# Rotary embedding over 16 heads: three matmul rows per tile in place of four, a new order of the first loads, and one last store

## Chip, cores, metric

One core of one Trainium2 chip. The metric is the device time of one execution in microseconds (us), median of several. A span is the time from the first to the last instruction in a trace of one execution; the device time of an execution was 1.8 us (kernel before) to 2.2 us (changed kernel) above its span. All runs quoted are fast, that is, none was over 1.5% above the fastest run of its kernel. The granted clock is the share of its full clock that TensorE was allowed, as the trace records it.

## The reference

Input x is 16 x 512 x 1024 fp32 (33.5 MB), seen as 16 heads of 64; cos and sin are 512 x 32.

```python
x = x.reshape(batch, seq, num_heads, head_dim)
x1, x2 = x[..., :half_dim], x[..., half_dim:]
rotated = concatenate([x1*cos - x2*sin, x1*sin + x2*cos], axis=-1)
```

So each output element is one product with cos plus one with a signed sin of the swapped half. Every byte is read once and written once: 67.1 MB.

## The kernel before

Eight tiles of 128 partitions x 8192 floats; a tile has eight "rows" k of 1024 floats per partition. Five tiles are buffered. For each row, POOL (GpSimd) makes `b` = swapped x times signed sin; VectorE (DVE) makes x times cos. The sum is made in one of two ways: in a matmul row, TensorE (PE) adds `b` onto the product in PSUM (the memory that matmuls accumulate in) by a multiplication with the identity and ScalarE (ACT) copies the sum back; in any other row DVE adds. In `own` rows DVE makes the sine product itself, in place, and PE adds that.

```python
PE_ROWS = (0, 2, 4, 6)          # matmul rows
DVE_B = ((0,), (0, 4))          # own rows in even and odd tiles
FIRST = (3, 8)                  # pieces of the first tile's load
LAST_OUT = (4, 8)               # pieces of the last tile's store
# ... (cut: views, pools)
load(0, 0, FIRST[0])
# sin table, then cos table (64 KB each), then the rest of tile 0, then tiles 1 to 4
# ... (cut)
nc.tensor.matmul(out=sin_t, lhsT=spread, rhs=sin_sb, start=True, stop=True)
nc.tensor.matmul(out=cos_t, lhsT=spread, rhs=cos_sb, start=True, stop=True)
nc.vector.tensor_scalar_mul(out=sns[:, :, 0, :], in0=sin_k, scalar1=-1.0)
nc.vector.tensor_copy(out=sns[:, :, 1, :], in_=sin_k)
# ... (cut: two more small sine copies)
for t in range(NT):
    for k in range(KK):
        r = xt[:, k * dim : (k + 1) * dim]
        own = k in DVE_B[t % 2]
        if not own:
            nc.gpsimd.tensor_tensor(out=halves(b), in0=swapped(r, nh), in1=over_heads(sk), op=ALU.mult)
        if k in PE_ROWS:
            nc.vector.tensor_tensor(out=pairs(ps), in0=pairs(r), in1=cos_b(k), op=ALU.mult)
            # own: DVE sine product in place; then two fp32 matmuls with the identity into ps
            nc.scalar.copy(out=r, in_=ps)
            while pending: add()
        else:
            while pending: add()
            nc.vector.tensor_tensor(out=pairs(ps), in0=pairs(r), in1=cos_b(k), op=ALU.mult)  # ps from pd, one buffer
            pending.append((r, ps, b))       # DVE's add comes later
    while pending: add()
    # store(t); the last tile in the pieces of LAST_OUT; loads of tiles 5 to 7 follow the store of tile 2
```

All loads and stores are issued by SyncE (SP) in the order loads 0 to 4, stores 0 to 2, loads 5 to 7, stores 3 to 7, on one queue (q1 of the profile, kind hardware_dynamic: 67.24 of the 67.28 MB). In the trace they landed in that order: store 0 at 62.4 us, store 2 at 82.3, load 5 at 92.0, load 7 at 111.4, store 3 at 122.0, store 6 at 150.9 and the second half of store 7 at 160.5.

Of the kernel before, what the change touches and what calls it, by code (L numbers as in the profile page):

```python
# [14 lines left out]
B_BUFS = 6  # L15
BANK = 512

PE_ROWS = (0, 2, 4, 6)

DVE_B = ((0,), (0, 4))  # L20

FIRST = (3, 8)
LAST_OUT = (4, 8)

SIN_PARTS = (64,)
COS_PARTS = (64,)


@with_exitstack
def kernel(  # L30
# [13 lines left out]
    nc = tc.nc  # L44
# [12 lines left out]
    cos_v = cos.rearrange("(p k) j -> p (k j)", k=KK)  # L57
    sin_v = sin.rearrange("(p k) j -> p (k j)", k=KK)
# [12 lines left out]
    def load(t, lo=0, hi=KK):  # L71
        if tiles[t] is None:
            tiles[t] = xp.tile([P, F], FP32, name="xt")
        s = slice(lo * dim, hi * dim)
        nc.sync.dma_start(out=tiles[t][:, s], in_=x_v[t][:, s])  # L75

    def store(t, lo=0, hi=KK):
        s = slice(lo * dim, hi * dim)
        nc.sync.dma_start(out=out_v[t][:, s], in_=tiles[t][:, s])

    load(0, 0, FIRST[0])
    sin_sb = bp.tile([P, dim], FP32, name="b")[:PB, : KK * half]
    cos_sb = bp.tile([P, dim], FP32, name="b")[:PB, : KK * half]
    for sb, v, parts in ((sin_sb, sin_v, SIN_PARTS), (cos_sb, cos_v, COS_PARTS)):
        lo = 0
        for hi in parts:
            nc.sync.dma_start(out=sb[lo:hi, :], in_=v[lo:hi, :])
            lo = hi
    for lo, hi in zip(FIRST, FIRST[1:]):
        load(0, lo, hi)  # L90
    for t in range(1, BUFS):
        load(t)
# [21 lines left out]
    nc.vector.tensor_copy(out=sns[:, :, 1, :], in_=sin_k)  # L114
    on_dve = sorted(set(DVE_B[0]) | set(DVE_B[1]))
    sns_t = tab[:, KK * half : KK * half + len(on_dve) * hd]
# [7 lines left out]
    def over_heads(s):  # L124
        return bass.AP(tensor=s.tensor, offset=s.offset, ap=[s.ap[0], [0, nh], [1, hd]])

    def swapped(r, n):
        return bass.AP(
            tensor=r.tensor, offset=r.offset + half, ap=[r.ap[0], [hd, n], [-half, 2], [1, half]]
        )  # L130
# [12 lines left out]
    def halves(r):  # L143
        return r.rearrange("p (h a j) -> p h a j", a=2, j=half)
# [7 lines left out]
    for t in range(NT):  # L152
        xt = tiles[t]
# [4 lines that stand above are left out]
                b = bp.tile([P, dim], FP32, name="b")  # L158
                sk = sns[:, k].rearrange("p a j -> p (a j)")
                nc.gpsimd.tensor_tensor(out=halves(b), in0=swapped(r, nh), in1=over_heads(sk), op=ALU.mult)  # L160
            if k in PE_ROWS:
                ps = pe.tile([P, dim], FP32, name="ps")
# [3 lines left out]
                for c in range(0, dim, BANK):  # L166
                    rhs = swapped(r[:, c : c + BANK], BANK // hd) if own else b[:, c : c + BANK]
                    nc.tensor.matmul(  # L168
                        out=ps[:, c : c + BANK], lhsT=ident, rhs=rhs, start=False, stop=True, skip_group_check=True
# [14 lines left out]
        else:  # L184
            lo = 0
            for hi in LAST_OUT:
                store(t, lo, hi)
                lo = hi
# [38 lines left out]
```

## Time and profile before

| what | value |
|---|---|
| time, median (first 3 runs) | 163.11 us |
| span of the profiled run | 161.6 us |
| moved | 67.28 MB, 416 GB/s over the span |
| busy: DVE, POOL, PE, ACT | 128.9, 121.0, 81.8, 33.7 us |
| first DVE row product / last DVE add ends | 10.96 / 142.96 us |
| last store issued / span ends | 143.03 / 161.6 us |

In the slices of the profile each digit is the busy share of one fortieth of the span in tenths. A line of a group or a timeline names source line, engine, operation, output<-input; in brackets stands the idle time before it and what ended it. `xt` is a tile of x, `b` a sine product, `ps` and `pd` are the PSUM buffers of matmul rows and of other rows, `tab` and `sns` hold the tables; SPq is SyncE's instruction queue. In a table of stretches the columns are the stretch, its length, busy us (and count) of PE, weight loads, DVE, ACT and POOL, then granted PE clock, DMA share and GB/s. The lines themselves are in the prediction.

### The profile page before, as it was taken

What the parts mean: (1) busy time and instruction counts of PE and PEld (TensorE: products, weight loads), DVE (VectorE), ACT (ScalarE), POOL (GpSimd) and SP (SyncE); (2) the same over time, 40 slices, a digit from 0 to 9 for tenths busy, and PEclk for the clock granted to TensorE, in tenths of its full rate; (3) what the DMA queues carried; (4) which work ended last, traced back from release to release, by engine and by line L of the source; (5) the groups of instructions that cost most, each with busy time, mean ns of one, the idle gap of its engine ahead of it and who ended that gap; (6) DMA issues with size and microseconds to landing.
All of it is one profiled execution on the core that took longest, in us unless ns stands there. A gap on an engine that the chain in (4) does not pass through costs nothing.

```text
span 161.6 us, 692 instructions
## 1 busy us (share of the span) xinstructions
PE 81.8 (51%) x136; PEld 30.3 (19%) x136; DVE 128.9 (80%) x115; ACT 33.7 (21%) x33; POOL 121.0 (75%) x58
## 2 busy tenths in 40 slices
PE   4136946496429742955097419660984194600000
PEld 1112301241114211311032114210321131100000
DVE  1059897999999989999999999999999999930000
ACT  0003242023302430223113302222223122220000
POOL 1049999999999999999994199999999997000000
PEclk9999996559975998799969965999689879995555
DMA  5999999999999999999999999999999999999992
GB/s 189 395 441 435 454 454 389 446 462 389 438 470 389 389 446 464 389 454 446 397 454 446 397 448 446 406 454 438 406 450 438 406 448 438 414 454 389 438 426 118
DMA packets 2756, 67.28 MB, mean 416 GB/s; under 512 B 320, under 2 KB 448, under 8 KB 448
## 3 DMA queue, kind: packets, MB, share of 16 engines
q1 hardware_dynamic: 2752, 67.24, 97.5%
q8 instruction: 1, 0.02, 0.0%
q14 instruction: 3, 0.02, 0.0%
HBM read 33.69 MB, written 33.55 MB: 416 GB/s over the span
## 4 chain that ended last, share of the span: by engine, by line
DVE 37%; PE 18%; issue 17%; POOL 6%; ACT 4%; DMA 4%; SPq 0%; DVEq 0%; ACTq 0%; POOLq 0%
PE ps L168 17%; DVE xt L150 12%; DVE pd L178 12%; DVE ps L163 7%; POOL b L160 6%; DVE xt L165 5%; ACT xt L171 4%; DMA b<-in_sin_dram 4%; PE tab L110 1%; PE tab L111 1%; DVE tab L118 0%; DVE sns L113 0%; SPq L75 0%; DVE sns L114 0%; DVEq L150 0%
## 5 line engine op out<-in xcount | busy, mean ns | idle before, releaser
L160 POOL TENSOR_TENSOR b<-xt,sns 128x1024 f32<-128x1024 f32 x52 | 120.3, 2350 | 14.5 <-DVE sns L114 9.2
L168 PE MATMUL ps<-xt,ident 128*128 128x512 f32 x48 | 35.8, 888 | 39.2 <-issue 24.5
L171 ACT COPY xt<-ps 128x1024 f32<-128x1024 f32 x32 | 32.4, 1012 | 95.2 <-PE ps L168 90.8
L168 PE MATMUL ps<-b,ident 128*128 128x512 f32 x80 | 43.5, 674 | 14.7 <-DVE ps L163 12.1
L150 DVE TENSOR_TENSOR xt<-pd,b 128x1024 f32<-128x1024 f32 x32 | 39.0, 1218 | 2.2 <-POOL b L160 1.1
L163 DVE TENSOR_TENSOR ps<-xt,tab 128x1024 f32<-128x1024 f32 x32 | 39.1, 1223 | 1.5 <-ACT xt L171 1.3
L178 DVE TENSOR_TENSOR pd<-xt,tab 128x1024 f32<-128x1024 f32 x32 | 39.3, 1227 | 0.8
L168 PEld LDWEIGHTS ps<-b,ident 128*128 128x128 f32 x80 | 17.1, 227 | 44.1 <-issue 30.6
L168 PEld LDWEIGHTS ps<-xt,ident 128*128 128x128 f32 x48 | 11.6, 267 | 58.8 <-issue 46.1
L165 DVE TENSOR_TENSOR xt<-xt,tab 128x1024 f32<-128x1024 f32 x12 | 14.6, 1220 | 0.4
L113 DVE TENSOR_SCALAR sns<-tab 128x256 f32<-128x256 f32 x1 | 0.4, 425 | 8.0 <-PE tab L111 8.0
L171 ACT ACT_TABLE_LOAD x1 | 1.3, 1283 | 13.5 <-DVE xt L165 13.5
L110 PE MATMUL tab<-b,spread 64*128 64x256 f32 x2 | 1.2, 697 | 4.5 <-DMA b<-in_sin_dram 4.5
L101 PE MATMUL ps<-zero 128*128 128x512 bf16 x4 | 1.9, 625 | 1.2 <-DVE zero L97 1.2
L110 PEld LDWEIGHTS tab<-b,spread 64*128 64x128 f32 x2 | 0.5, 308 | 5.4 <-issue 5.4
L111 PE MATMUL tab<-b,spread 64*128 64x256 f32 x2 | 1.1, 631 | 0.0
L97 DVE MEMSET zero<- 128x256 uint32 x1 | 0.3, 272 | 0.9 <-PEq L208 0.9
L101 PEld LDWEIGHTS <-zero 128*128 128x128 bf16 x4 | 0.4, 129 | 1.7 <-DVE zero L97 1.2
L111 PEld LDWEIGHTS tab<-b,spread 64*128 64x128 f32 x2 | 0.7, 333 | 0.2
L118 DVE COPY tab<-sns 128x64 f32<-128x64 f32 x2 | 0.5, 228 | 0.1
L109 DVE COPY spread<-ident 64x64 f32<-64x64 f32 x2 | 0.3, 182 | 0.2 <-POOL ident masks.py:199 0.2
masks.py:197 POOL MEMSET ident<- 128x128 f32 x1 | 0.2, 204 | 0.3 <-POOLq L208 0.3
(6 smaller groups left out, 1.1 us busy)
## 6 DMA issues: line engine op xcount, KB each, us to landing
xt<-in_x_dram SPq DMA_DIRECT2D x7, 4096.0 KB, 29.5
out_dram<-xt SPq DMA_DIRECT2D x7, 4096.0 KB, 30.3
out_dram<-xt SPq DMA_DIRECT2D x2, 2048.0 KB, 18.1
xt<-in_x_dram SPq DMA_DIRECT2D x1, 2560.0 KB, 11.3
xt<-in_x_dram SPq DMA_DIRECT2D x1, 1536.0 KB, 6.2
b<-in_sin_dram SPq DMA_DIRECT2D x1, 64.0 KB, 6.3
b<-in_cos_dram SPq DMA_DIRECT2D x1, 64.0 KB, 6.1
```

The lines of the kernel that those rows point to most:

```text
L101: nc.tensor.matmul(out=ps[:, c : c + BANK], lhsT=zero[:, :P], rhs=zero, start=True, stop=True)
L110: nc.tensor.matmul(out=sin_t, lhsT=spread, rhs=sin_sb, start=True, stop=True)
L111: nc.tensor.matmul(out=cos_t, lhsT=spread, rhs=cos_sb, start=True, stop=True)
L113: nc.vector.tensor_scalar_mul(out=sns[:, :, 0, :], in0=sin_k, scalar1=-1.0)
L118: nc.vector.tensor_copy(out=sns_t[:, i * hd : (i + 1) * hd], in_=sns[:, k])
L150: nc.vector.tensor_tensor(out=r, in0=ps, in1=b, op=ALU.add)
L160: nc.gpsimd.tensor_tensor(out=halves(b), in0=swapped(r, nh), in1=over_heads(sk), op=ALU.mult)
L163: nc.vector.tensor_tensor(out=pairs(ps), in0=pairs(r), in1=cos_b(k), op=ALU.mult)
L165: nc.vector.tensor_tensor(out=halves(r), in0=halves(r), in1=swapped_signed(k), op=ALU.mult)
L168: nc.tensor.matmul(out=ps[:, c : c + BANK], lhsT=ident, rhs=rhs, start=False, stop=True, skip_group_check=True)
L171: nc.scalar.copy(out=r, in_=ps)
L178: nc.vector.tensor_tensor(out=pairs(ps), in0=pairs(r), in1=cos_b(k), op=ALU.mult)
```

## The change

The rows that go over PE fall from four to three, the pieces of the first load are made smaller with the tables placed between them (seemingly to let work start sooner), and the last tile is stored whole.

```diff
-PE_ROWS = (0, 2, 4, 6)
-DVE_B = ((0,), (0, 4))
-FIRST = (3, 8)
-LAST_OUT = (4, 8)
-SIN_PARTS = (64,)
-COS_PARTS = (64,)
+PE_ROWS = (0, 3, 6)
+DVE_B = ((0,), (0, 3))
+FIRST = (2, 4, 8)
+LAST_OUT = (8,)
@@ after load(0, 0, FIRST[0]) and the two table buffers
-    for sb, v, parts in ((sin_sb, sin_v, SIN_PARTS), (cos_sb, cos_v, COS_PARTS)):
-        ... (one DMA each)
-    for lo, hi in zip(FIRST, FIRST[1:]):
+    nc.sync.dma_start(out=sin_sb, in_=sin_v)
+    load(0, FIRST[0], FIRST[1])
+    nc.sync.dma_start(out=cos_sb, in_=cos_v)
+    for lo, hi in zip(FIRST[1:], FIRST[2:]):
         load(0, lo, hi)
```

More of the change, by code (lines that the diff above doesn't have):

```diff
@@ L83 @@
     cos_sb = bp.tile([P, dim], FP32, name="b")[:PB, : KK * half]
-    for sb, v, parts in ((sin_sb, sin_v, SIN_PARTS), (cos_sb, cos_v, COS_PARTS)):
-        lo = 0
-        for hi in parts:
-            nc.sync.dma_start(out=sb[lo:hi, :], in_=v[lo:hi, :])
-            lo = hi
-    for lo, hi in zip(FIRST, FIRST[1:]):
+    nc.sync.dma_start(out=sin_sb, in_=sin_v)
+    load(0, FIRST[0], FIRST[1])
+    nc.sync.dma_start(out=cos_sb, in_=cos_v)
+    for lo, hi in zip(FIRST[1:], FIRST[2:]):
         load(0, lo, hi)
```

## The prediction

> **What bounds the kernel now.** I read the page's slices first, because a kernel that only loads, rotates and stores must be either limited by its transfers or by its busiest engine.
>
> ```profile
> DVE  1059897999999989999999999999999999930000
> POOL 1049999999999999999994199999999997000000
> PEclk9999996559975998799969965999689879995555
> DMA  5999999999999999999999999999999999999992
> ```
>
> VectorE (DVE) is busy 80% of the span but does nothing in the last four and a half slices (some 18 us); the transfers are at 9 in every slice but the first and the last. So the bound is transfers: 67.28 MB at about 430 GB/s. The page's chain of waits gives 37% to DVE and 17% to PE; it ends with the last add at 142.96 us and says nothing of the 18.6 us after it, so I don't take it for the bound.
>
> Next the waits of the DMA queue's own engine, and the busy table of chosen stretches:
>
> ```profile
> SPq L79 <- DVE xt L150: 111.5, 8, 21.0
> SPq L75 <- DMA out_dram<-xt: 19.9, 3, 9.8
> SPq L222 <- DMA out_dram<-xt: 17.1, 1, 17.1
> ```
> ```profile
> 143.00:158.60 15.60, 0.00 (x0) 0.00 (x0) 0.00 (x0) 0.00 (x0) 0.00 (x0) 0.57 0.98 419
> 148.90:158.60 9.70, 0.00 (x0) 0.00 (x0) 0.00 (x0) 0.00 (x0) 0.00 (x0) 0.50 0.99 422
> 100.00:143.00 43.00, 24.53 (x44) 8.55 (x43) 41.92 (x36) 12.14 (x12) 36.15 (x16) 0.91 1.00 433
> ```
>
> The last store is issued at 143.03 and the queue then waits 17.1 us for it. Summing the GB/s after 143 us in 1 us pieces gives 6.62 MB still to move. One tile is 4.19 MB, so 2.43 MB of tile 6 is still ahead of tile 7's first byte: at 425 GB/s that takes 5.7 us, to about 148.8 us. That is the number on which everything turns: **the queue runs dry at about 149 us unless tile 7 has been issued by then**. Before, its last half was issued 6 us (plus its first half, 5 us more) ahead of need.
>
> Last, the pace of DVE in tile 7 (start, duration; steps are start to start) and the start of the program:
>
> ```profile
> 126.11 1.22 DVE L163 TENSOR_TENSOR ps<-xt,tab 128x1024 f32<-128x1024 f32 x1
> 127.36 1.22 DVE L165 TENSOR_TENSOR xt<-xt,tab 128x1024 f32<-128x1024 f32 x1
> 128.50 1.22 DVE L178 TENSOR_TENSOR pd<-xt,tab 128x1024 f32<-128x1024 f32 x1
> 129.63 1.22 DVE L163 TENSOR_TENSOR ps<-xt,tab 128x1024 f32<-128x1024 f32 x1
> 130.76 1.22 DVE L150 TENSOR_TENSOR xt<-pd,b 128x1024 f32<-128x1024 f32 x1
> 132.01 1.23 DVE L178 TENSOR_TENSOR pd<-xt,tab 128x1024 f32<-128x1024 f32 x1
> ...
> 140.40 1.23 DVE L178 TENSOR_TENSOR pd<-xt,tab 128x1024 f32<-128x1024 f32 x1
> 141.74 1.22 DVE L150 TENSOR_TENSOR xt<-pd,b 128x1024 f32<-128x1024 f32 x1
> ```
> ```profile
> 7.57 1.19 PE L110 MATMUL tab<-b,spread 64*128 64x256 f32 x2 [4.49 <-DMA b<-in_sin_dram]
> ...
> 8.55 1.06 PE L111 MATMUL tab<-b,spread 64*128 64x256 f32 x2
> 9.65 0.42 DVE L113 TENSOR_SCALAR sns<-tab 128x256 f32<-128x256 f32 x1 [8.02 <-PE tab L111]
> ...
> 10.96 1.23 DVE L163 TENSOR_TENSOR ps<-xt,tab 128x1024 f32<-128x1024 f32 x1
> ```
>
> The reader sees four kinds of step: 1.14 us to an instruction that needs nothing of the one before; 1.25 to a product that overwrites pd just after the add that read it; 1.26 from the cosine product to the in-place sine product of the same row; 1.34 from a product in pd to the add that reads it at once. At the start, the first sine copy (L113) waits for the matmul of the cos table (L111), not for that of the sine table that it reads.
>
> [...] the trace has 1215 to 1230 for all four groups. So a further add is no cheaper than a product. [...] the trace has 433 in mid-run[...]. Here the first load (1.57 MB) lands 6.2 us after its issue at 0.73; at the 418 GB/s of those microseconds its bytes take 3.76, so 2.4 us are fixed[...]. In a full queue this hides behind the neighbour; behind an empty queue it is paid.
>
> **The change, part by part.**
>
> *Rows.* A row on PE costs DVE one product; a row off PE costs a product and an add. Rows on PE go from (0,2,4,6) to (0,3,6): one more add per tile, 8 in all. The rows whose sine product DVE does itself stay at one in even and two in odd tiles, so that group stays at 12 and POOL at 52. PE loses 16 of its 128 accumulating matmuls and ACT 8 of 32 copies; neither sets the end. In DVE's new order (even tile: product, own sine product, then product, add, product, product, add, product, add, product, product, add, product, add) I count the steps:
> - Before, even: 8 x 1.14 + 3 x 1.25 + 1.26 + 1.34 = 15.47; odd has one own product more, 1.26: 16.73. Tile 7 by this rule ends 16.81 after its start; measured 142.96 - 126.11 = 16.85.
> - After, even: 6 x 1.14 + 4 x 1.25 + 1.26 + 3 x 1.34 = 17.12; odd 18.38. With two neighbouring rows off PE the add follows its own product at once, three times per tile and not once: so a tile costs 1.65 more, not one bare 1.14.
> - Four pairs: before 4 x 32.20 = 128.8, after 4 x 35.50 = 142.0.
>
> Before, the real walk from 10.96 to 142.96 has 132.0, 3.1 above the count: 1.45 in tile 0 (waits for POOL and ACT), the rest spread. POOL makes a product each 2.31 us; in tile 0 after the change its row 7 is ready some 16.2 us after its start, and DVE wants it at about 16.4 after that same moment. So I expect little waiting there, and 0.3 us in all.
>
> *Start.* The cos table lands at 1.75 + 6.1 = 7.85 now, behind 1.57 MB of x. After, it stands behind 2.10 MB: 0.52 MB / 0.42 = 1.25 us later, so 9.1. The sine table is sooner by the same, but L113 will still wait for the cos matmul if the waits are as now (the built program's waits are the same). Then 0.12 + about 1.1 for the matmul, 10.3; the four copies and gaps take 1.31 (9.65 to 10.96), so the first product starts at 11.65: 0.7 later. The smaller first piece gains nothing as DVE has nothing to do without the tables.
>
> *DVE's end.* 11.65 + 142.0 + 0.1 (the last one's duration in place of its step) + 0.3 = about 153.9, against 142.96.
>
> *The tail.* The queue is dry from 148.9. The last tile now goes in one store of 4.19 MB, issued at 153.95. 2.4 fixed + 4.19/0.42 = 10.0 gives landing at 166.3; the span ends 1.1 after the landing (160.5 to 161.6 now): 167.4. Time less span is 163.11 - 161.6 = 1.5, so 168.9. [...] I take 168.8. Dropping the split of the last tile costs nothing before, but here it means that 2 MB that are ready about 9 us earlier wait for the rest.
>
> **The rivals.** (a) All stays hidden: transfers remain the bound, 163.1, perhaps less by a few tenths for a smoother start. For it: 97.5% of transfer time, and 18 us of idle DVE at the end. Against: those 18 us consist of 6 of earlier backlog and 10 of the tile itself, so slack is 6, and the count says 11. It would need the extra add to be eaten by waits now there; only 3.1 us of them exist. (b) The naive count: 8 adds x 1.14 = 9.1, all present waits gone, and the start better, not worse (the sine copy freed from the cos matmul, -0.7): end of DVE at about 149.5, time about 164.5. Against: the wait seen at L113 and the 1.34 steps. (c) POOL becomes the bound: its row products take 7 x 2.31 = 16.2 against 17.1 in an even tile. It would add waits: 170 to 171. For: it is close; against: in odd tiles it has only 13.9 of 18.4, so it gets ahead by up to six buffers. (d) Earlier stores starve the queue in mid-run: tile 2 would end at about 64 and is needed at about 72; tile 6 at 135 and needed near 139. So no.
>
> **Range and chances.** DVE's end may err by 1 either way, the tail by 0.7: 167.0 to 170.6. The 2% line is 166.4; to stay below it DVE must end before 151.5, which needs (b) in large part: 0.09. Faster by 2%[...]: 0.01. Slower: 0.90.
>
> **What would show it.** DVE busy near 138.7 us (128.9 + 8 x 1.22), first row product at 11.6, last add ending near 153.9; even tiles of 17.1 and odd of 18.4; three steps of 1.34 per tile; a dip of the DMA share to zero between about 149 and 155; the last store landing some 12.4 us after its issue. If the dip is absent, (a) was right; if the first product starts near 10.3, the wait on the cos matmul was misread; if DVE idles on POOL in mid-run, (c).

Where the prediction is marked as cut, it used rules and figures that no trace or run of this case shows. With them went its step from the measured 433 GB/s to a rate that can't be exceeded, which was not shown. Its sum for the time came to 166.3 + 1.1 + 1.5 = 168.9 us, and all terms of that sum are still there; a second sum, made with figures of the cut kind, is cut, and the 168.8 was taken a little below the first. That the fixed part of a store hides in a full queue is in the trace of the kernel before: its ten whole-tile transfers from store 0 to store 6 landed 9.5 to 10.6 us after one another, where 4.19 MB at 433 GB/s take 9.7; behind an empty queue the changed kernel's last store landed 11.1 us after its issue. The 1215 to 1230 are the ns of one DVE row instruction.

## The result and the profile after

The changed kernel takes 169.82 us (169.1 to 170.23, 6 runs) against 163.13 (163.08 to 163.17, 6 runs): ratio 1.0406, 95% interval 1.0383 to 1.0428. A ratio here is the mean time of one kernel's fast runs over that of the other's in the same rounds, so not quite the quotient of the medians quoted. The profiled run has a span of 167.8 us, 6.2 more than before.

The slices of the changed kernel:

```profile
DVE  1039999999999899999999999999999999997000
PEclk9999995585855595555678955765555985585855
DMA  5999999999999999999999999999999999930885
```

DVE is now busy until slice 37 and the DMA row has a hole, "30" in slices 36 and 37, that the kernel before had nowhere. The PEclk row has far more fives; that comes back below. The same hole in the table of stretches of the changed kernel:

```profile
148.00:149.00 1.00, 0.17 (x1) 0.00 (x0) 0.97 (x2) 0.79 (x1) 0.00 (x0) 1.00 0.39 164
149.00:156.00 7.00, 3.57 (x4) 1.00 (x4) 5.33 (x5) 1.24 (x2) 0.00 (x0) 0.76 0.00 0
156.00:165.00 9.00, 0.00 (x0) 0.00 (x0) 0.00 (x0) 0.00 (x0) 0.00 (x0) 0.61 1.01 433
```

Within 148 to 149 us the transfers end, for seven microseconds nothing moves, then the last tile goes at 433 GB/s. The waits of the queue's own engine between 130 and 168 us:

```profile
SPq L76 <- DVE xt L145: 33.4, 2, 18.0
SPq L217 <- DMA out_dram<-xt: 10.8, 1, 10.8
SPq L76 <- ACT xt L166: 1.1, 1, 1.1
```

Before, the final wait was 17.1 us for a store that stood in line; now it is 10.8, the store alone. The last line was not predicted: after DVE's last add, the store waits 1.1 us more for ACT. The timeline at that place (start, duration):

```profile
150.90 3.57 PE L163 MATMUL ps<-b,ident 128*128 128x512 f32 x4 [2.73 <-DVE ps L158]
...
153.25 1.23 DVE L145 TENSOR_TENSOR xt<-pd,b 128x1024 f32<-128x1024 f32 x1
154.55 1.01 ACT L166 COPY xt<-ps 128x1024 f32<-128x1024 f32 x1 [5.33 <-PE ps L163]
155.59 0.33 SPq L76 DMA_DIRECT2D out_dram<-xt  x1
```

The matmuls of row 6 take 3.57 us, so ACT's copy of that row ends at 155.57, after the add (154.48). And the start of the changed kernel, to be held against the start shown in the prediction:

```profile
9.68 1.22 PE L106 MATMUL tab<-b,spread 64*128 64x256 f32 x2 [2.44 <-DMA b<-in_cos_dram]
10.93 0.42 DVE L108 TENSOR_SCALAR sns<-tab 128x256 f32<-128x256 f32 x1 [9.30 <-PE tab L106]
...
12.24 1.23 DVE L158 TENSOR_TENSOR ps<-xt,tab 128x1024 f32<-128x1024 f32 x1
```

The sine copy L108 waits for the cos matmul, which waits for the cos table behind 2.1 MB of x. DVE's first product is 1.28 us later than before.

The steps of the last tile (first five instructions):

```profile
136.04 1.22 DVE L158 TENSOR_TENSOR ps<-xt,tab 128x1024 f32<-128x1024 f32 x1
137.29 1.22 DVE L160 TENSOR_TENSOR xt<-xt,tab 128x1024 f32<-128x1024 f32 x1
138.43 1.22 DVE L173 TENSOR_TENSOR pd<-xt,tab 128x1024 f32<-128x1024 f32 x1
139.76 1.23 DVE L145 TENSOR_TENSOR xt<-pd,b 128x1024 f32<-128x1024 f32 x1
141.02 1.23 DVE L173 TENSOR_TENSOR pd<-xt,tab 128x1024 f32<-128x1024 f32 x1
```

The steps from start to start are 1.25, 1.14, 1.33, 1.26: an add that follows its own product at once starts 1.33 after it, close to the 1.34 counted. The last even tile takes 17.08 us (118.96 to 136.04), the last odd one 18.44 to the end of its last add.

### The profile page after: what moved, and what is told of

The parts are those of the page before. It is cut to its first block, busy times and chain, and to the rows that moved or that the text cites. A ratio compares the mean times of both kernels' runs of the same rounds, so it can differ in the third digit from the quotient of the medians.

```text
span 167.8 us, 612 instructions
## 1 busy us (share of the span) xinstructions
PE 84.4 (50%) x104; PEld 26.4 (16%) x104; DVE 139.6 (83%) x123; ACT 25.6 (15%) x25; POOL 121.4 (72%) x58
## 4 chain that ended last, share of the span: by engine, by line
DVE 70%; issue 13%; DMA 4%; PE 3%; SPq 1%; ACT 1%; DVEq 0%; ACTq 0%
DVE pd L173 28%; DVE xt L145 23%; DVE ps L158 10%; DVE xt L160 9%; DMA b<-in_cos_dram 4%; PE ps L163 2%; PE tab L106 1%; ACT xt L166 1%; SPq L72 1%; SPq L81 0%; DVEq L145 0%; DVE tab L113 0%; DVE sns L108 0%; DVE sns L109 0%; DVEq L160 0%
## 5 line engine op out<-in xcount | busy, mean ns | idle before, releaser
L163 PE MATMUL ps<-xt,ident 128*128 128x512 f32 x48 | 42.8, 1045 | 34.1 <-issue 20.1
L163 PE MATMUL ps<-b,ident 128*128 128x512 f32 x48 | 37.3, 922 | 29.3 <-DVE ps L158 18.7
L145 DVE TENSOR_TENSOR xt<-pd,b 128x1024 f32<-128x1024 f32 x40 | 48.9, 1221 | 2.9 <-DVE pd L173 0.5
L173 DVE TENSOR_TENSOR pd<-xt,tab 128x1024 f32<-128x1024 f32 x40 | 49.1, 1228 | 1.1
L166 ACT COPY xt<-ps 128x1024 f32<-128x1024 f32 x24 | 24.3, 1012 | 115.2 <-PE ps L163 105.2
L158 DVE TENSOR_TENSOR ps<-xt,tab 128x1024 f32<-128x1024 f32 x24 | 29.3, 1222 | 0.0
L163 PEld LDWEIGHTS ps<-xt,ident 128*128 128x128 f32 x48 | 13.4, 307 | 62.1 <-issue 57.4
L163 PEld LDWEIGHTS ps<-b,ident 128*128 128x128 f32 x48 | 11.6, 266 | 55.6 <-POOL b L155 30.9
L108 DVE TENSOR_SCALAR sns<-tab 128x256 f32<-128x256 f32 x1 | 0.4, 423 | 9.3 <-PE tab L106 9.3
```

Of the source, the lines that this page charges most:

```text
L145: nc.vector.tensor_tensor(out=r, in0=ps, in1=b, op=ALU.add)
L163: nc.tensor.matmul(out=ps[:, c : c + BANK], lhsT=ident, rhs=rhs, start=False, stop=True, skip_group_check=True)
```

## The experiments

**Theory A:** the time is set by the queue. As long as the last store is issued before the queue runs dry, compute is free; once it comes later, each microsecond counts, and with one whole-tile store the delay is that of the last row. **Rival B:** compute is the bound, and the time follows DVE's end whatever the stores look like. **Rival C:** one store of 4 MB is by itself worse than two of 2 MB. Twelve kernels ran; all gave right results. Here is what they left (issue is that of the last store; times are medians, the ratio is to the kernel before):

| run | first product | last add ends | last store issued | span | time | ratio [95%] |
|---|---|---|---|---|---|---|
| x2, before + one last store | 11.04 | 142.86 | 142.92 | 161.4 | 163.06 | 0.9987 [0.9972, 1.0002] |
| x5, before + new load order | 12.26 | 144.59 | 144.66 | 162.1 | 163.54 | 1.0014 [0.9998, 1.003] |
| x3, before + three rows | 10.90 | 152.75 | 152.92 | 160.8 | 163.33 | 1.0002 [0.9985, 1.002] |
| x4, before + three rows + one store | 11.04 | 152.89 | 153.65 | 165.8 | 167.89 | 1.0288 [1.0269, 1.0308] |
| x1, after + two halves | 12.47 | 154.76 | 157.22 | 164.5 | 165.18 | 1.0129 [1.0074, 1.0184] |
| after_again | 12.52 | 154.81 | 155.75 | 167.9 | 169.71 | 1.0402 [1.0377, 1.0427] |
| x6, after + sine copies first | 10.84 | 153.11 | 154.41 | 166.7 | 168.76 | 1.0327 [1.0289, 1.0365] |
| x7, after + rows 0, 3, 5 | 12.28 | 154.24 | 154.30 | 166.5 | 168.54 | 1.0326 [1.031, 1.0342] |
| x9, after, four rows in tiles 4 to 7 | 12.35 | 147.75 | 147.81 | 161.6 | 163.48 | 1.0016 [1.0001, 1.0032] |
| x8, after + pieces of 3, 3, 2 | 12.52 | 154.80 | 155.93 | 161.3 | 163.31 | 1.0003 [0.999, 1.0016] |
| x10, after + x6 + x7 + two halves | 11.47 | 153.33 | 153.40 | 161.3 | 163.23 | 1.0012 [0.9995, 1.0029] |
| x11, after + spare matmuls | 12.30 | 154.57 | 154.63 | 166.8 | 168.68 | 1.0345 [1.0319, 1.0371] |

Row by row the table already decides most: in all five runs with one late whole-tile store (x4, after_again, x6, x7, x11) the span ends 12.15 to 12.3 us after that store is issued; in all others, x1 apart, it ends at 160.8 to 162.1 whatever DVE does. Against the ranges written down before the runs, the medians of x4, x7, x8 and x9 came out lower by 0.31, 0.06, 0.09 and 0.02 us, those of x1, x5 and x6 higher by 0.18, 0.14 and 0.06; each lies nearer to the range of theory A, or of the term that it tests, than to the alternative.

### One part at a time (x1 to x4)

x1, the changed kernel with the last store in halves:

```diff
-LAST_OUT = (8,)
+LAST_OUT = (4, 8)
```

> The changed kernel, with its last tile stored in two halves again. Theory A (the queue runs dry at about 149 us because the whole last tile is held back for its last row): the first half can go at about 149.2, the second at 155.6 with 2.1 MB behind it, so landing near 161.7 and a time of 164.4 to 165.0; the add pace and the end of VectorE (154.5) stay as they are. Rival B (whatever VectorE's end is, the time follows it, 15 us later): stays at 169.8.

Measured 165.18. The three runs without a full profile have 164.34 to 165.18; the profiled one has 166.67 and is odd. Its record says that the clock was granted in full, a mean of 1.000, yet its matmuls are the slowest of all runs:

```profile
L163 PE MATMUL ps<-b,ident 128*128 128x512 f32 x48 | 59.9, 1407 | 9.6 <-DVE ps L158 6.0 <-POOL b L155 3.5
L163 PE MATMUL ps<-xt,ident 128*128 128x512 f32 x48 | 59.5, 1397 | 16.4 <-ACT xt L166 7.0 <-DVE xt L160 5.3 <-issue 4.1
```

In the changed kernel the same two groups have means of 922 and 1045 ns. With such slow matmuls row 3 and row 6 were copied late, and the halves went only at 151.04 and 157.22. So 4 to 5 of the 6.7 us are won back by storing in halves although DVE ends no sooner (154.76): against B. What remains is that the first half, too, waits for a matmul row (row 3) and comes after the queue is dry. In this profile it came 2 us after that; at the matmul times of the changed kernel's own profile, where the copy of row 3 ends at 149.22, it would come only just after. The other three runs kept no trace that shows it.

x2, the kernel before with one last store:

```diff
-LAST_OUT = (4, 8)
+LAST_OUT = (8,)
```

> The kernel before, with its last tile in one store. Theory A: the store is issued at 143.0, 6 us before the queue would run dry, so 163.1, unchanged within 0.5. Rival C (one store of 4 MB in place of two of 2 MB is by itself the loss): 167 or more.

Measured 163.06, ratio 0.9987. Rival C is out: an unsplit store costs nothing if it is in time.

x3, the kernel before with the rows alone:

```diff
-PE_ROWS = (0, 2, 4, 6)
-DVE_B = ((0,), (0, 4))
+PE_ROWS = (0, 3, 6)
+DVE_B = ((0,), (0, 3))
```

> The kernel before with three matmul rows alone; loads and the two halves of the last store as before. VectorE should end at 153.2 (10.96 + 142.2), 10.2 later than before. Theory A: the first half covers the queue until about 154 and the second half is issued at 153.2 to 154.3, so 163.1 to 164.2. Rival B: 168.5.

Measured 163.33, ratio 1.0002. DVE's end moved by 9.8 us, to 152.75, and the time did not move at all: B is out.

x4, x3 and x2 together:

> The kernel before with three matmul rows and the single last store, with the old order of the loads. VectorE ends at 153.2, the store is issued there or up to 1.1 later (copy of row 6). Theory A: 1.3 below the changed kernel, 168.2 to 168.7, so that the order of the tables is worth 1.3 of the loss. If the order of the loads doesn't matter, 169.8.

Measured 167.89, a little below what was expected. Neither part costs anything alone; together they cost 4.7. Its last store is issued 1.94 us before the changed kernel's (153.65 against 155.59), of which the first product gives 1.2, a shorter wait for ACT 0.3, DVE's walk the rest; the spans differ by 2.0.

### The terms of the start and of the end (after_again, x6, x7, x9)

> The changed kernel again, unedited, as the base for the runs beside it on the same chip: 169.1 to 170.2, its last store issued about 1 us after the last add because the copy of row 6 ends later.

Measured 169.71 (169.45 to 170.17): repeated on another occasion, with the wait for ACT again (store at 155.75, last add ended 154.81).

x6, the order of two small steps:

```diff
 nc.tensor.matmul(out=sin_t, lhsT=spread, rhs=sin_sb, start=True, stop=True)
-nc.tensor.matmul(out=cos_t, lhsT=spread, rhs=cos_sb, start=True, stop=True)
 # ... four sine copies on DVE ...
+nc.tensor.matmul(out=cos_t, lhsT=spread, rhs=cos_sb, start=True, stop=True)
```

> The changed kernel with the cos matmul moved behind the four sine copies, so that those wait for the sine matmul alone. If the first product waits for the sine copies, which wait for the cos matmul (the term of the start in the prediction), it starts near 10.9 in place of 12.2 and the time falls by 1.3, to 168.0 to 168.7. If the start is set by the first loads or by POOL instead, no change.

The timeline of this run has

```profile
10.84 1.23 DVE L158 TENSOR_TENSOR ps<-xt,tab 128x1024 f32<-128x1024 f32 x1 [2.14 <-PE tab L113]
```

so the first product came directly after the cos matmul, 1.7 us sooner than in after_again and 1.4 sooner than in the profiled changed kernel. The time is 168.76, ratio 1.0327 against 1.0402 for after_again: 1.2 us by the ratios, 0.95 by the medians, against 1.3 expected. Its last store still waited for ACT, by 1.3 us (154.41 against the add's 153.11). The wait of the sine copies for the cos matmul was real, and came from the order of the source: with nothing but that order changed, the first sine copy starts at about 7.42 in place of 10.93. That is an estimate: the 10.84 above, less the 2.14 of idle time, less the 1.28 that the four copies take in the changed kernel; the sine matmul of this run ends at 7.38.

x7, another third row:

```diff
-PE_ROWS = (0, 3, 6)
+PE_ROWS = (0, 3, 5)
```

> The changed kernel with the matmul rows at 0, 3, 5 in place of 0, 3, 6: the same number of VectorE instructions and the same count of each kind of step, so VectorE still ends near 154.5, but the last matmul row is copied well ahead of it. If the last store waits 1.1 us for ScalarE's copy of row 6 behind slow matmuls, that wait goes: 168.6 to 169.0, and its runs spread less. If it doesn't matter: 169.8.

Its end in the timeline:

```profile
151.07 1.01 ACT L166 COPY xt<-ps 128x1024 f32<-128x1024 f32 x1 [1.72 <-PE ps L163]
...
153.01 1.23 DVE L145 TENSOR_TENSOR xt<-pd,b 128x1024 f32<-128x1024 f32 x1
154.30 0.33 SPq L76 DMA_DIRECT2D out_dram<-xt  x1
```

DVE ends at 154.24, but ACT has been done for 2 us and the store goes at once. Measured 168.54, 1.2 below after_again, and the runs lie within 0.23 us where those of after_again spread over 0.72. In the profiled runs the store goes 1.45 us sooner, of which 0.24 is an earlier first product and 0.33 a shorter walk of DVE; the wait for ACT was worth the rest, about 0.9. That it also made the spread is not shown: there are four runs of each, and x11, whose profiled run has no such wait, spreads over 1.36.

x9, three rows in half of the tiles:

```diff
-PE_ROWS = (0, 3, 6)
-DVE_B = ((0,), (0, 3))
+PE_ROWS = 4 * ((0, 3, 6),) + 4 * ((0, 2, 4, 6),)
+DVE_B = 2 * ((0,), (0, 3)) + 2 * ((0,), (0, 4))
```

(with the lookups by tile t, and a third small sine copy, as row 4 is an own row too.)

> The changed kernel with three matmul rows in tiles 0 to 3 alone, four in tiles 4 to 7, still one last store and the new order of the loads. VectorE's end by the counts: 12.2 + 2 x 35.5 + 2 x 32.2 and about 1 of waits = 148.5. Theory A (slack of about 6, then a bend): the store goes just as the queue runs dry, so only its fixed start shows: 163.5 to 164.6. A loss in proportion to the rows moved (half of 6.7) would give 166.5.

DVE ends 4.8 us later than in the kernel before, and the last store is one piece. The time is 163.48, ratio 1.0016; the final wait of the queue's engine in this run:

```profile
SPq L217 <- DMA out_dram<-xt: 12.4, 1, 12.4
```

It lies between 17.1 (before) and 10.8 (after): the slack is nearly used up, but not overdrawn. The loss is not in proportion to the rows moved (that would have been 166.5). With the 12.2 us from issue to the span's end, a single last store should, by this estimate, begin to cost at 161.6 - 12.2 = 149.4 us, in agreement with x9 (147.81, free) and x4 (153.65, 4.2 us of span).

### The rest of the change, the repair, and the clock (x5, x8, x10, x11)

x5, the new load order in the kernel before (the load part of the diff above):

> The kernel before with the new order of the loads and tables alone (four matmul rows, last store in halves). Its first product should start at 12.2 to 12.5 in place of 10.96, VectorE's end 1.3 to 1.5 later, at about 144.4. Theory A (a last store issued before about 149.4 costs nothing): 163.0 to 163.4, no change. If every microsecond of the start shows at the end: 164.5.

The first product came at 12.26, DVE's end at 144.59, and the time was 163.54, ratio 1.0014 with an interval that includes 1 (the expected 163.4 was just missed). On its own the start's loss is hidden.

x8, the changed kernel with finer last stores:

```diff
-LAST_OUT = (8,)
+LAST_OUT = (3, 6, 8)
```

> The changed kernel with its last tile in pieces of 3, 3 and 2 rows. Theory A: the first piece goes at 145.8, before the queue is dry, the second at about 152 just before that one is through, the third at 155.6 with 1.05 MB: 163.4 to 164.0, with VectorE's end unchanged at 154.5. If the loss comes from the late last add as such: 169.8.

Measured 163.31, ratio 1.0003: the whole loss is gone although DVE ends at 154.80 and the last piece goes only at 155.93. The stretch that was empty is now full:

```profile
149.00:156.00 7.00, 3.57 (x4) 1.17 (x4) 5.66 (x5) 1.92 (x2) 0.00 (x0) 0.61 0.95 401
```

x10, the three repairs together (the edits of x1, x6 and x7):

> The changed kernel with three repairs: sine copies ahead of the cos matmul, rows 0, 3, 5, last store in two halves. VectorE ends at about 153.2, second half issued there, while the first half still moves until about 153.6. Theory A: the transfers are the bound again, 163.0 to 163.6; nothing gained over the kernel before, as that one has no dry stretch to win back.

Measured 163.23, ratio 1.0012. As expected it is level with the kernel before and not better; no version tried beats that one.

x11 asks why row 6's matmuls were so slow. It gives PE more to do:

```diff
+spare = pfix.tile([P, BANK], FP32)
@@ rows off PE
 pending.append((r, ps, b))
+nc.tensor.matmul(out=spare, lhsT=ident, rhs=b[:, :BANK], start=True, stop=True)
```

> The changed kernel with one more accumulating-free matmul per row off PE into a spare bank, whose result nobody reads, so that PE has more to do and shorter gaps. If the lower granted clock (0.69 against 0.83) comes from PE being idle more often, the mean clock rises to 0.8 or more, row 6's four matmuls take 2 to 2.5 us in place of 3.6, its copy ends before the last add, and the time falls by about 1, to 168.5 to 169.0. If the clock is lower because something else limits it, it stays at 0.7 or falls and the time stays at 169.7 or rises.

The mean granted clocks of the profiled runs, changed kernel and then x11 (kernel before: 0.833):

```profile
core 0: 167.8 us, clock 0.686
```
```profile
core 0: 166.8 us, clock 0.885
```

And row 6 of the last tile in x11:

```profile
151.00 2.41 PE L164 MATMUL ps<-b,ident 128*128 128x512 f32 x4 [2.45 <-DVE ps L159]
```

Useless work raised the granted clock in all four runs (0.872 to 0.898, against 0.646 to 0.695 in after_again), the same matmuls took 2.41 in place of 3.57 us, ACT was done by 154.50, just before the last add (154.57), and the time fell to 168.68 (one of the four runs, that with the lowest clock of them, took 169.63). So the lower clock of the changed kernel goes with PE having less to do (104 matmuls against x11's 184), not with a limit from too much. By what rule the clock is granted, the runs do not show.

## Why the prediction was right, point by point

- *The queue runs dry at about 149 us.* Confirmed: it did so between 148 and 149, and stood still until after 155.6. This is the step on which the result rests, and x3, x2 and x4 show that, with the old order of the loads, it takes both a late end of DVE and the unsplit store. With the new order two halves still lost 1.3% (x1); three pieces lost nothing (x8).
- *Tile times of 17.12 and 18.38, end of DVE at 153.9.* Measured 17.08 and 18.44 in the last two tiles and an end of 154.48. From the first product to the end it was 142.24 against 142.4 predicted. The waits present before did go, but the 1.33 steps used that up. DVE was busy 139.6, against 138.7. A slip in the sum hardly mattered: its terms, 11.65 + 142.0 + 0.1 + 0.3, give 154.05 and not 153.9.
- *Start at 11.65.* 12.24: the mechanism (sine copies wait for the cos matmul) is shown by x6, the size fell short by 0.6. The cos table landed at 2.36 + 7.3 = 9.66, not 9.1; why the 0.5 more was not looked into.
- *Store issued at once after the last add.* This failed: it waited 1.1 us for ACT's copy of row 6, whose matmuls took 3.57 us in a run with a mean clock of 0.686 (0.833 before). The prediction said of PE and ACT that "neither sets the end" (and counted 16 matmuls fewer where the profile has 32 fewer, 96 for 128); x7 and x11 show that together they do, by about 1 us.
- *13.5 us from issue to the end of the span.* Too much: 12.2 in five runs. The fixed part, 2.4, was read from the program's first load. The last store landed 155.59 + 0.33 + 10.8 = 166.7, so 11.1 after its issue; with 4.19 MB at the 433 GB/s of that stretch (9.7) the fixed part is 1.4, an estimate. The end of the span followed 1.1 later, as predicted.
- *Time less span, 1.5.* It was 2.2 for the profiled run of the changed kernel, and 1.8 for the kernel before when both numbers are of the same run: the prediction had set a median of one kind of run against a span of another.

These errors, +0.6, +1.1, -1.3 and +0.7, partly cancel: the 169.82 measured lies 1.0 above the 168.8 predicted. That the wait for ACT and the too large fixed part of the store offset each other is luck; the dry queue and the late start are not. Of the rivals, (a) "stays hidden" holds for each part alone, but not for the whole; (b) and (c) did not happen. For (b) the present waits did go, but the start was later and not sooner, and the longer steps came (its own terms, 142.96 + 9.1 - 3.1 - 0.7, give 148.3 and not 149.5). For (c), in mid-run DVE has a single step lengthened by 0.4 (56.18 to 57.92; why was not looked into), and from 74 us on POOL waited for DVE, not DVE for POOL.

What stays open: the full-clock record beside slow matmuls in the profiled run of x1 (1.000, with means of 1397 to 1407 ns against 922 to 1045 at a recorded 0.686; nothing here tests whether the record is at fault), and why the changed kernel's time exceeds its span by more than before (1.9 to 2.2 in its first six runs, against 1.8).

## What to carry to other kernels

In a kernel bound by one transfer queue, ask not how much longer compute takes but how much backlog the queue has when the last tile becomes ready. In these runs a change of compute was free up to that slack (x3, x5, x9: ratios 1.0002 to 1.0016), and beyond it each microsecond counted (x4, x6, x7: the span ended 12.15 to 12.3 us after the last store's issue). Store the last tile in pieces so that only the last piece waits for the last row; here three pieces were worth the whole loss (x8: ratio 1.0003 in place of 1.0402), and splitting cost nothing where it wasn't needed (x2: 163.06 unsplit, 163.28 split). And an engine relieved of work isn't simply faster: here PE with fewer rows ran at a lower clock (0.686 against 0.833) and held the last store back (by 1.1 us).
